# Merge stage of a hybrid encoder layer: stores one pass later, own buffers for three weight slabs, output-stage input in the raw weight buffers

## The chip, the core and the metric

The kernel runs on one core of a Trainium2 chip. The metric is device time in microseconds (us) of one execution, input and output in the chip's main memory (HBM). The engines are called as the profile calls them: PE multiplies matrices, DVE and POOL do elementwise work, ACT does activations and copies, and SP issues every transfer (DMA) that is spoken of here.

## What is computed

One layer of a streaming encoder, 2048 tokens of width 1024, all in 32-bit floats. Three branches (attention "fox", a state-space layer "s5", a cross-attention "mem") give gated outputs `y_fox`, `y_s5`, `y_mem`. The end of the layer is what this case is about:

```python
gates = sigmoid(gl + b_merge).reshape(Bn, L, N_BRANCH, D_MODEL)
merged = (gates[:, :, 0] * (y_fox @ w_proj_fox)
          + gates[:, :, 1] * (y_s5 @ w_proj_s5)
          + gates[:, :, 2] * (y_mem @ w_proj_mem))
x = x + merged @ w_out
return rms_norm(x, g_final)
```

To keep accuracy each 32-bit operand is split into a rounded part (hi) and the rest (lo), and each product is three matmuls: hi by hi, hi by lo, lo by hi.

## The kernel before

The tokens are cut into four chunks of 512 (c = 3, 2, 1, 0), the 1024 output channels into eight blocks of 128 (m). Between the stages everything lies in scratch tensors in HBM: `s_ys`, `s_ym`, `s_yx` are the three branches' outputs, `s_gl` the gates, `s_mg` the merged rows, `s_mp` a partial sum of chunk 3.

- **Chunk 3** (`gen_merge0`) is merged while the attention runs on, as filler for PE. It goes in two parts: part 0 merges s5 and mem into `s_mp`; part 1, when the attention is nearly over, adds the fox branch, with the partial loaded back (line 950), and stores to `s_mg` (line 953). Gates and reloaded partials share two buffers named `g`. Its last line loads chunk 2's ten `ys` and `ym` tiles through two raw buffers named `yr` and splits them (`merge_load`, line 905 for the load).
- **Chunks 2, 1, 0** (`merge_out`) follow in 24 passes, one per chunk and m. A pass has 48 matmuls of 128x512: 18 for s5 into a bank psB, 12 for mem into psC, 18 for fox into psA, with three weight slabs: two of 640 columns (`w_proj`, slabs 0 and 1) and one of 768 (`w_proj_x`). DVE multiplies each bank by its gate (line 977), POOL adds the three (lines 978, 979), SP stores the sum (line 980). Within the passes the next chunk's sixteen y tiles are loaded, and in chunk 0's passes `w_out` (line 990).
- **The output stage** takes 16 blocks of 128 tokens: load eight merged tiles `mt` (line 1000), split, 48 matmuls with `w_out` into psF and psA in turn, add the residual `xo` (line 1013), norm, store.

A slab is loaded by `load_w` into one of two raw buffers `wraw` (line 139), then split: hi by ACT or POOL (`split`, lines 891 and 893, chosen by the flag `hi_act`), lo by DVE (line 895). All three slabs of a pass go through the same two `wraw`; slabs 0 and 1 share two split buffers, the third has two of its own. `hi_act` is set at the start of `merge_out`.

The order on each engine is made at build time by a scheduler, which follows the program's order, the free buffers and its own estimate of durations. SP's list is one queue: a transfer that waits for a buffer or for a result holds back every transfer behind it.

Of the kernel before, what the change touches and what calls it, by code (L numbers as in the profile page):

```python
# [4 lines left out]
F32 = mybir.dt.float32  # L5
F32R = mybir.dt.float32r
# [6 lines left out]
D = 1024  # L13
L = 2048
NC = 4
CW = 512
KD = 8
# [10 lines left out]
NV = 268  # L28
# [21 lines left out]
class Layer:  # L50
# [863 lines left out]

    def merge_w(self, m, part, pool=None):
        return [self.load_w(self.i["w_proj"][2 * m + a], (5, 128)) for a in range(2)] if part == 0 else \
            [self.load_w(self.i["w_proj_x"][m], (6, 128), pool)]

    def gen_merge0(self):


        nc, s, c = self.nc, self.s, NC - 1
        self.yp, self.close_yp = self.pool("yp", side="left")
        self.ys = {q: [] for q in range(NC)}
        self.merge_load(c, self.SRC[:10], self.yp, self.yp)
        ys = self.ys[c]
        for part, brs in ((0, ((1, range(6)), (2, range(6, 10)))), (1, ((0, range(10, 16)),))):
            if part:
                while not self.ready:
                    yield  # L930
                self.merge_load(c, self.SRC[10:], self.yp, self.yp)
            for m in range(KD):
                ms = slice(m * 128, (m + 1) * 128)
                ws = self.merge_w(m, part)
                g = []
                for br, ks in brs:
                    t = self.merge_gate(self.yp, br, m, c, 2)
                    ps = self.psFA() if self.over else self.psF()
                    for kk in ks:
                        w = ws[0 if part else kk // 5]  # L940
                        q = (kk - 10) if part else kk % 5
                        self.mm3(ps, (w[0][:, q, :], w[1][:, q, :]), ys[kk], kk == ks[0], kk == ks[-1])
                        if kk % 2 and kk != ks[-1]:
                            yield
                    nc.vector.scalar_tensor_tensor(out=t, in0=t, scalar=1.0, in1=ps, op0=ALU.add, op1=ALU.mult)
                    g.append(t)
                    yield
                if part:
                    t = self.yp.tile([128, CW], F32, tag="g", name="g", bufs=2)
                    nc.sync.dma_start(out=t, in_=s["mp"][ms, :])  # L950
                    g.append(t)
                nc.gpsimd.tensor_add(g[0], g[0], g[1])
                nc.sync.dma_start(out=s["mg"][ms, c * CW:(c + 1) * CW] if part else s["mp"][ms, :], in_=g[0])
        self.merge_load(c - 1, self.SRC[:10], self.yp, self.yp)

    def merge_out(self):
        nc, s, i = self.nc, self.s, self.i
        p, close = self.pool("mrg", side="right")
        gfin = p.tile([128, D], F32, name="gfin")
        nc.sync.dma_start(out=gfin, in_=i["g_final"].partition_broadcast(128))  # L960
        yq, yp = p, self.yp
        self.hi_act = True
        pm, close_m = self.pool("mrw", side="right")
        self.merge_load(NC - 2, self.SRC[10:], yq, pm, 3)
        for c in range(NC - 2, -1, -1):
            ys = self.ys[c]
            for m in range(KD):
                ps = {0: self.psA(), 1: self.psB(), 2: self.psC()}
                ws = self.merge_w(m, 0) + self.merge_w(m, 1, pm)
                cnt = {0: 6, 1: 6, 2: 4}  # L970
                for kk, (n, k, br) in enumerate(self.SRC):
                    w, q = ws[min(kk // 5, 2)], kk - 5 * min(kk // 5, 2)
                    self.mm3(ps[br], (w[0][:, q, :], w[1][:, q, :]), ys[kk], k == 0, k == cnt[br] - 1)
                g = {}
                for br in (1, 2, 0):
                    t = g[br] = self.merge_gate(pm, br, m, c)
                    nc.vector.scalar_tensor_tensor(out=t, in0=t, scalar=1.0, in1=ps[br], op0=ALU.add, op1=ALU.mult)
                nc.gpsimd.tensor_add(g[1], g[1], g[2])
                nc.gpsimd.tensor_add(g[1], g[0], g[1])
                nc.sync.dma_start(out=s["mg"][m * 128:(m + 1) * 128, c * CW:(c + 1) * CW], in_=g[1])  # L980
                if c and m < KD - 1:
                    for e in self.SRC[m * 16 // 7:(m + 1) * 16 // 7]:
                        self.merge_load(c - 1, [e], yq if (e[0] == "yx") == (c == 1) else yp, pm, 3)
                elif m < KD - 1:
                    if m == 0:
                        wo, nw = {}, 0
                    for _ in range((8 * (m + 1)) // 7 - (8 * m) // 7):
                        n, q = nw // 4, nw % 4
                        raw = self.wp.tile([128, 4 * NV], F32, tag="wraw", name="wraw", bufs=2)
                        nc.sync.dma_start(out=raw[:, :1024], in_=i["w_out"][nw])  # L990
                        for a in range(2):
                            w = (yq if 2 * nw + a < 10 else yp).tile([128, 1024], F32R, tag="y", name="wo", bufs=16)
                            self.split(w[:, :512], w[:, 512:], raw[:, a * 512:(a + 1) * 512])
                            wo[n, 2 * q + a] = (w[:, :512], w[:, 512:])
                        nw += 1
        close_m()
        po, close_o = self.pool("mro", side="right")
        for t in [c * 4 + q for c in range(NC - 1, -1, -1) for q in range(4)]:
            m_c = po.tile([128, KD, 128], F32, tag="m", name="mt", bufs=2)
            nc.sync.dma_start(out=m_c, in_=s["mg"].rearrange("(k p) n -> p k n", p=128)[:, :, t * 128:(t + 1) * 128])  # L1000
            hi = self.wp.tile([128, KD, 128], F32R, tag="whi", name="whi", bufs=2)
            lo = self.wp.tile([128, KD, 128], F32R, tag="wlo", name="wlo", bufs=2)
            self.split(hi, lo, m_c)
            x = po.tile([128, D], F32, tag="x", name="xo", bufs=3)
            nc.sync.dma_start(out=x, in_=i["x"][t * 128:(t + 1) * 128, :])
            j = po.tile([128, D], F32, tag="j", name="jo", bufs=2)
            ssq, r = (po.tile([128, 2], F32, tag=q, name=q, bufs=2) for q in ("ssq", "rs"))
            for n in range(2):
                ns = slice(n * 512, (n + 1) * 512)
                ps = self.psFA()  # L1010
                for k in range(KD):
                    self.mm3(ps, (hi[:, k, :], lo[:, k, :]), wo[n, k], k == 0, k == KD - 1)
                nc.vector.scalar_tensor_tensor(out=x[:, ns], in0=ps, scalar=0.5, in1=x[:, ns], op0=ALU.mult, op1=ALU.add)
                nc.scalar.activation(j[:, ns], x[:, ns], AF.Square, accum_out=ssq[:, n:n + 1])
            nc.vector.tensor_add(ssq[:, 0:1], ssq[:, 0:1], ssq[:, 1:2])
            self.rsqrt(po, r[:, 0:1], ssq[:, 0:1], 1)
            for n in range(2):
                ns = slice(n * 512, (n + 1) * 512)
                nc.vector.scalar_tensor_tensor(out=j[:, ns], in0=x[:, ns], scalar=r[:, 0:1], in1=gfin[:, ns],
                                               op0=ALU.mult, op1=ALU.mult)  # L1020
                nc.sync.dma_start(out=self.out[t * 128:(t + 1) * 128, ns], in_=j[:, ns])
        close_o()
        close()
        self.close_yp()

    def run(self):
# [20 lines left out]
        for n, _ in enumerate(fox):  # L1047
            marks.append(self.pe)
            due += PACE
            while due >= 1.0:  # L1050
# [3 lines left out]
                        next(fill, None)  # L1054
                else:
                    next(fill, None)
        self.over = True
        for _ in fill:
            pass
        self.close_f()  # L1060
# [77 lines left out]
```

## Time and profile before

| | |
|---|---|
| time, median of 3 | 3053.83 us (3053.64 to 3059.55) |
| the profiled execution | 3062.09 us, its span 3060.3 us |
| granted PE clock, mean | 0.991 |
| DMA | 417.80 MB, mean 137 GB/s |

The views are read as follows. A table by stage gives the engines' busy time, with the number of instructions in brackets, the granted PE clock, the DMA engines' busy share and the rate. Since matmuls overlap, their number in a stage says more of PE than its busy time. The list of waits says who waited for whom. The chain of work is followed back from the last instruction; its pieces stand in order of time.

### The profile page before, as it was taken

What the parts mean: (1) busy time and instruction counts of PE and PEld (TensorE: products, weight loads), DVE (VectorE), ACT (ScalarE), POOL (GpSimd) and SP (SyncE); (2) the same over time, 40 slices, a digit from 0 to 9 for tenths busy, and PEclk for the clock granted to TensorE, in tenths of its full rate; (3) what the DMA queues carried; (4) which work ended last, traced back from release to release, by engine and by line L of the source; (5) the groups of instructions that cost most, each with busy time, mean ns of one, the idle gap of its engine ahead of it and who ended that gap; (6) DMA issues with size and microseconds to landing.
All of it is one profiled execution on the core that took longest, in us unless ns stands there. A gap on an engine that the chain in (4) does not pass through costs nothing.

```text
span 3060.3 us, 43643 instructions
## 1 busy us (share of the span) xinstructions
PE 2968.6 (97%) x14656; PEld 2420.4 (79%) x14656; DVE 1845.9 (60%) x4982; ACT 1030.9 (34%) x2023; POOL 877.9 (29%) x1186
## 2 busy tenths in 40 slices
PE   9999999999999999999999999999999998999899
PEld 7889977777777778888878888888887776777687
DVE  5333389899985763322217777777777886434344
ACT  5102111111112321222216666666666542222222
POOL 0010000000002432122116565556655763222100
PEclk9999999999999999999999999999999999999999
DMA  5343323323335655344353434444444548766542
GB/s 167 107 138 95 104 88 114 116 93 115 129 124 157 176 153 169 118 127 125 116 160 101 128 117 111 121 120 112 114 117 132 161 137 269 223 184 212 168 144 97
DMA packets 306671, 417.80 MB, mean 137 GB/s; under 512 B 84084, under 2 KB 165236, under 8 KB 306436
## 3 DMA queue, kind: packets, MB, share of 16 engines
q1 hardware_dynamic: 306160, 414.95, 45.4%
q8 instruction: 116, 1.90, 0.3%
q14 instruction: 107, 0.88, 0.1%
q10 hardware_dynamic: 288, 0.07, 0.0%
HBM read 276.00 MB, written 138.90 MB: 136 GB/s over the span
## 4 chain that ended last, share of the span: by engine, by line
PE 76%; DMA 10%; DVE 6%; issue 3%; POOL 3%; ACT 2%; SPq 1%; POOLq 0%; DVEq 0%; ACTq 0%
PE psF L147 10%; PE psF L148 10%; PE psF L149 10%; PE psA L148 7%; PE psA L147 7%; PE psA L149 7%; PE psC L799 5%; PE psB L783 5%; PE psA L752 2%; PE psA L751 2%; PE psC L149 2%; DMA wraw<-in_w_proj 2%; PE psC L148 2%; PE psC L147 2%; DMA wraw<-in_w_proj_x 1%
## 5 line engine op out<-in xcount | busy, mean ns | idle before, releaser
L147 PE MATMUL psF<-hh,whi 128*128 128x512 f32 (+1 forms) x1160 | 468.9, 404 | 5.4 <-DVE elo L228 2.5
L149 PE MATMUL psF<-hh,wlo 128*128 128x512 f32 (+1 forms) x1160 | 460.0, 397 | 0.0
L148 PE MATMUL psF<-hl,whi 128*128 128x512 f32 (+1 forms) x1160 | 459.5, 396 | 0.0
L895 DVE TENSOR_TENSOR wlo<-wraw,whi 128x1024 fp32r<-128x1024 f32 (+2 forms) x216 | 250.9, 1163 | 307.5 <-POOL whi L893 156.5
L893 POOL TENSOR_SCALAR whi<-wraw 128x1024 fp32r<-128x1024 f32 (+2 forms) x144 | 145.7, 1012 | 728.5 <-PE psA L148 315.3
L147 PE MATMUL psA<-hh,whi 128*128 128x512 f32 (+1 forms) x816 | 321.7, 396 | 1.7 <-ACT hh L187 1.0
L148 PE MATMUL psA<-hl,whi 128*128 128x512 f32 (+1 forms) x816 | 323.2, 396 | 0.0
L149 PE MATMUL psA<-hh,wlo 128*128 128x512 f32 (+1 forms) x816 | 321.1, 394 | 0.6 <-DVE wlo L895 0.6
L799 PE MATMUL psC<-Pt,v 128*128 128x512 f32 x864 | 266.5, 398 | 6.1 <-DVE Pt L787 4.2
L787 DVE TENSOR_TENSOR Pt<-psB,Pt 128x512 fp32r<-128x512 f32 x336 | 226.0, 685 | 73.3 <-ACT Pt L786 70.7
L147 PEld LDWEIGHTS psF<-hh,whi 128*128 128x128 f32 x1160 | 219.0, 189 | 52.1 <-DVE elo L228 3.3
L149 PEld LDWEIGHTS psF<-hh,wlo 128*128 128x128 f32 x1160 | 218.6, 188 | 51.3 <-issue 0.4
L148 PEld LDWEIGHTS psF<-hl,whi 128*128 128x128 f32 x1160 | 219.1, 189 | 45.8 <-issue 0.4
L753 DVE CUSTOM_DVE_ANT_0 P<-psA,nf 128x512 f32<-128x512 f32 (+1 forms) x336 | 201.4, 627 | 45.7 <-PE psA L752 26.5
L786 ACT CAST Pt<-psB 128x512 fp32r<-128x512 f32 x336 | 191.6, 586 | 96.2 <-PE psB L783 51.6
L762 POOL TENSOR_SCALAR P<-P,rd 128x768 f32<-128x768 f32 (+1 forms) x240 | 193.8, 824 | 57.2 <-DVE rd L759 36.4
L751 PE MATMUL psA<-kk,qh 128*128 128x512 f32 (+1 forms) x480 | 184.9, 390 | 6.0 <-DVE mx L753 3.6
L147 PEld LDWEIGHTS psA<-hh,whi 128*128 128x128 f32 x816 | 153.5, 189 | 37.1 <-POOL whi L893 1.8
L149 PEld LDWEIGHTS psA<-hh,wlo 128*128 128x128 f32 x816 | 153.9, 189 | 35.4 <-DVE wlo L895 0.8
L799 PEld LDWEIGHTS psC<-Pt,v 128*128 128x128 f32 x864 | 153.1, 189 | 34.9 <-DVE Pt L787 8.7
L148 PEld LDWEIGHTS psA<-hl,whi 128*128 128x128 f32 x816 | 154.0, 189 | 33.6 <-DVE hl L188 0.2
L783 PE MATMUL psB<-ident,P 128*128 128x128 f32 x1200 | 176.9, 274 | 0.3 <-POOL P L762 0.2
(356 smaller groups left out, 6193.8 us busy)
## 6 DMA issues: line engine op xcount, KB each, us to landing
wraw<-in_w_in SPq DMA_DIRECT2D x90, 512.0 KB, 4.2
s_gl<-ehi SPq DMA_DIRECT2D x96, 256.0 KB, 2.6
g<-s_gl SPq DMA_DIRECT2D x96, 256.0 KB, 4.8
wraw<-in_w_proj SPq DMA_DIRECT2D x64, 320.0 KB, 3.3
s_vs<-ev_v SPq DMA_DIRECT2D x48, 256.0 KB, 2.7
nf<-s_nf SPq DMA_DIRECT2D x24, 512.0 KB, 6.7
v<-s_vs SPq DMA_DIRECT2D x24, 512.0 KB, 6.2
qh<-s_qh SPq DMA_DIRECT2D x96, 128.0 KB, 3.9
```

What stands on the lines that cost most here:

```text
L147: nc.tensor.matmul(out, a[0], b[0], start=first, stop=False)
L148: nc.tensor.matmul(out, a[0], b[1], start=False, stop=False)
L149: nc.tensor.matmul(out, a[1], b[0], start=False, stop=last)
L751: nc.tensor.matmul(ps[:, :wm], q[0][:, qs], kk[:, c0:c0 + wm], start=True, stop=False)
L753: nc.vector.tensor_tensor_reduce(out=pr[:, c * 512:c * 512 + w], in0=ps[:, :w], in1=nf[:, c0:c0 + w], scale=1.0, scalar=-3.0e38, op0=ALU.a ...
L762: nc.gpsimd.tensor_scalar(out=c, in0=c, scalar1=rd, scalar2=0.5, op0=ALU.mult, op1=ALU.mult)
L783: nc.tensor.transpose(ps[:, o:o + 128], P[b][:, kt * 128:(kt + 1) * 128], self.ident)
L786: nc.scalar.copy(hi, psv)
L787: nc.vector.tensor_sub(lo, psv, fl32(hi))
L799: self.pe = nc.tensor.matmul(o, v, m, start=(kt == 0), stop=(kt == 2 * G + 1))
L893: self.nc.gpsimd.tensor_scalar(out=hi, in0=x, scalar1=sc, scalar2=1.0, op0=ALU.mult, op1=ALU.mult)
L895: self.nc.vector.tensor_sub(lo, x, fl32(hi))
```

## The change

`merge_out` gets its slabs from a new function: slab 0 as before by `wraw`, slabs 1 and x through two raw buffers of their own (`raw`) into split buffers of their own, two for each slab. Its sums are stored by `store()` at the end of the next pass. It has six gate buffers in place of five, and two `yr` buffers in place of three. `gen_merge0` stores part 1's sums one m later, and loads the partials back into `yr` in place of `g`. `hi_act` is set when the attention ends, before the rest of `gen_merge0` is written. The tiles `mt` use the `wraw` buffers, and `gfin` is loaded at the start of the output stage.

```diff
+    def merge_ws(self, m, p):
+        ws = [self.load_w(self.i["w_proj"][2 * m], (5, 128))]
+        for src, k, t in ((self.i["w_proj"][2 * m + 1], 5, "b"), (self.i["w_proj_x"][m], 6, "x")):
+            raw = p.tile([128, 768], F32, tag="raw", name="raw", bufs=2)[:, :k * 128]
+            self.nc.sync.dma_start(out=raw, in_=src)
+            hi, lo = (p.tile([128, k * 128], F32R, tag=n + t, name=n + t, bufs=2) for n in ("hi", "lo"))
+            self.split(hi, lo, raw)
+            ws.append(tuple(x.rearrange("p (k m) -> p k m", k=k) for x in (hi, lo)))
+        return ws
...
 # gen_merge0
-                    t = self.yp.tile([128, CW], F32, tag="g", name="g", bufs=2)
+                    t = self.yp.tile([128, CW], F32, tag="yr", name="yr", bufs=2)
                     nc.sync.dma_start(out=t, in_=s["mp"][ms, :])
...
-                nc.sync.dma_start(out=s["mg"][ms, c * CW:(c + 1) * CW] if part else s["mp"][ms, :], in_=g[0])
+                if last:
+                    nc.sync.dma_start(out=last[0], in_=last[1])
+                if part:
+                    last = s["mg"][ms, c * CW:(c + 1) * CW], g[0]
+                else:
+                    nc.sync.dma_start(out=s["mp"][ms, :], in_=g[0])
+        nc.sync.dma_start(out=last[0], in_=last[1])
         self.merge_load(c - 1, self.SRC[:10], self.yp, self.yp)
...
 # merge_out
-        gfin = p.tile([128, D], F32, name="gfin")
-        nc.sync.dma_start(out=gfin, in_=i["g_final"].partition_broadcast(128))
-        self.hi_act = True
-        self.merge_load(NC - 2, self.SRC[10:], yq, pm, 3)
+        self.merge_load(NC - 2, self.SRC[10:], yq, pm)
...
-                ws = self.merge_w(m, 0) + self.merge_w(m, 1, pm)
+                ws = self.merge_ws(m, pm)
...
-                    t = g[br] = self.merge_gate(pm, br, m, c)
+                    t = g[br] = self.merge_gate(pm, br, m, c, 6)
...
-                nc.sync.dma_start(out=s["mg"][m * 128:(m + 1) * 128, c * CW:(c + 1) * CW], in_=g[1])
+                store()
+                last = slice(m * 128, (m + 1) * 128), slice(c * CW, (c + 1) * CW), g[1]
...
+        store()
         close_m()
         po, close_o = self.pool("mro", side="right")
+        gfin = po.tile([128, D], F32, name="gfin")
+        nc.sync.dma_start(out=gfin, in_=i["g_final"].partition_broadcast(128))
...
-            m_c = po.tile([128, KD, 128], F32, tag="m", name="mt", bufs=2)
+            m_c = self.wp.tile([128, 4 * NV], F32, tag="wraw", name="mt", bufs=2)[:, :1024].rearrange("p (k n) -> p k n", k=KD)
...
 # run
-        self.over = True
+        self.over = self.hi_act = True
         for _ in fill:
             pass
```

**SP, one pass of chunk 1**, without y loads, before:

```order
L980 DMA s_mg<-g 128x512
L912 DMA g<-s_gl 128x512 x2
L139 DMA wraw<-in_w_proj_x 128x768
L139 DMA wraw<-in_w_proj 128x640
L912 DMA g<-s_gl 128x512
L139 DMA wraw<-in_w_proj 128x640
```

And of the change, where `raw` are the new raw buffers:

```order
L983 DMA s_mg<-g 128x512
L912 DMA g<-s_gl 128x512 x2
L139 DMA wraw<-in_w_proj 128x640
L924 DMA raw<-in_w_proj 128x640
L912 DMA g<-s_gl 128x512
L924 DMA raw<-in_w_proj_x 128x768
```

The number of transfers is the same. The store in the list is now that of an earlier pass, and two of the three slabs have left `wraw`.

**SP, the turn from chunk 3 to chunk 2**, with buffer numbers, which rise with the place in the program: before, `yr_26302` to `yr_26347` are chunk 2's ten `ys` and `ym` tiles, and `g_26074` is the first of chunk 3's eight partials that is loaded back.

```order
L905 DMA yr_26312<-s_ys_133 128x512
L905 DMA yr_26317<-s_ys_133 128x512
L139 DMA wraw_26110<-in_w_proj_x 128x768
L808 DMA s_yx_131<-oo_25859 64x256
L773 DMA gf_25941<-s_gf_122 64x256
L905 DMA yr_26322<-s_ys_133 128x512
L905 DMA yr_26327<-s_ys_133 128x512
L953 DMA s_mp_135<-g_25976 128x512
L912 DMA g_26052<-s_gl_124 128x512
L139 DMA wraw_26142<-in_w_proj_x 128x768
L950 DMA g_26074<-s_mp_135 128x512
```

Of the change: `yr_26297` is the last of the partials, `yr_26302` chunk 2's first `ys` tile and `yr_26307` to `yr_26327` the other five; `yr_26470` to `yr_27031` are chunk 1's tiles.

```order
L961 DMA yr_26297<-s_mp_135 128x512
L139 DMA wraw_26665<-in_w_proj 128x640
L924 DMA raw_26671<-in_w_proj 128x640
L905 DMA yr_26561<-s_ys_133 128x512
L905 DMA yr_26566<-s_ys_133 128x512
L912 DMA g_26275<-s_gl_124 128x512
L965 DMA s_mg_136<-g_26243 128x512
L905 DMA yr_26302<-s_ys_133 128x512
L905 DMA yr_26652<-s_ys_133 128x512
L905 DMA yr_26657<-s_ys_133 128x512
L970 DMA s_mg_136<-g_26275 128x512
L905 DMA yr_26307<-s_ys_133 128x512
```

Chunk 2's `ys` tiles stood ahead of the first reloaded partial and now stand behind the last one, with pairs of chunk 1's tiles between them; `yr_26327`, the sixth, stands two further pairs of chunk 1's tiles below the last row shown. PE's list has turned to fit: between the last run of five attention matmuls (line 799) and the first matmul into psB there were 156 merge matmuls, and now there are 228, since the fox sums of three passes and the whole of chunk 3 stand ahead of psB.

**SP, the end of the merge**, before:

```order
L990 DMA wraw<-in_w_out 128x1024
L980 DMA s_mg<-g 128x512
L139 DMA wraw<-in_w_proj 128x640
L912 DMA g<-s_gl 128x512 x2
L139 DMA wraw<-in_w_proj 128x640
L139 DMA wraw<-in_w_proj_x 128x768
L912 DMA g<-s_gl 128x512
L980 DMA s_mg<-g 128x512 x2
L1000 DMA mt<-s_mg 128x8x128
```

Of the change:

```order
L1023 DMA mt<-s_mg 128x8x128
L912 DMA g<-s_gl 128x512
L983 DMA s_mg<-g 128x512
L912 DMA g<-s_gl 128x512 x2
L1023 DMA mt<-s_mg 128x8x128
L983 DMA s_mg<-g 128x512
L1023 DMA mt<-s_mg 128x8x128
L983 DMA s_mg<-g 128x512
L1020 DMA gfin<-in_g_final 128x1024
L1028 DMA xo<-in_x 128x1024 x3
```

Three `mt` loads (and a fourth, further up) have moved ahead of the last store; `gfin` and the residuals `xo` stay behind it.

More of the change, by code (lines that the diff above doesn't have):

```diff
@@ L916, in merge_w @@
         return [self.load_w(self.i["w_proj"][2 * m + a], (5, 128)) for a in range(2)] if part == 0 else \
-            [self.load_w(self.i["w_proj_x"][m], (6, 128), pool)]
+            [self.load_w(self.i["w_proj_x"][m], (6, 128))]
+    def merge_ws(self, m, p):
[7 more added lines that the diff above has]
+        return ws
     def gen_merge0(self):
@@ L925, in gen_merge0 @@
         self.merge_load(c, self.SRC[:10], self.yp, self.yp)
-        ys = self.ys[c]
+        ys, last = self.ys[c], None
         for part, brs in ((0, ((1, range(6)), (2, range(6, 10)))), (1, ((0, range(10, 16)),))):
@@ L958, in merge_out, with store @@
         p, close = self.pool("mrg", side="right")
-        gfin = p.tile([128, D], F32, name="gfin")
-        nc.sync.dma_start(out=gfin, in_=i["g_final"].partition_broadcast(128))
         yq, yp = p, self.yp
-        self.hi_act = True
         pm, close_m = self.pool("mrw", side="right")
-        self.merge_load(NC - 2, self.SRC[10:], yq, pm, 3)
+        self.merge_load(NC - 2, self.SRC[10:], yq, pm)
+        last = None
+        def store():
+            if last:
+                nc.sync.dma_start(out=s["mg"][last[0], last[1]], in_=last[2])
         for c in range(NC - 2, -1, -1):
@@ L979, in merge_out @@
                 nc.gpsimd.tensor_add(g[1], g[0], g[1])
-                nc.sync.dma_start(out=s["mg"][m * 128:(m + 1) * 128, c * CW:(c + 1) * CW], in_=g[1])
+                store()
+                last = slice(m * 128, (m + 1) * 128), slice(c * CW, (c + 1) * CW), g[1]
                 if c and m < KD - 1:
                     for e in self.SRC[m * 16 // 7:(m + 1) * 16 // 7]:
-                        self.merge_load(c - 1, [e], yq if (e[0] == "yx") == (c == 1) else yp, pm, 3)
+                        self.merge_load(c - 1, [e], yq if (e[0] == "yx") == (c == 1) else yp, pm)
                 elif m < KD - 1:
```

## The prediction, made before the changed kernel was run

> **What bounds the kernel.** First the page, for the span and the engine that fills it:
>
> ```profile
> span 3060.3 us, 43643 instructions
> PE 2968.6 (97%) x14656; PEld 2420.4 (79%) x14656; DVE 1845.9 (60%) x4982; ACT 1030.9 (34%) x2023; POOL 877.9 (29%) x1186
> ```
>
> PE bounds the whole, so a change can only win where PE stands still. The second view is the table by stage, over the part that the change touches:
>
> ```profile
> 2340.00:2520.00 180.00, 166.13 (x860) 132.76 (x858) 149.36 (x374) 94.00 (x199) 126.29 (x168) 0.99 0.51 149
> 2520.00:2560.00 40.00, 29.52 (x102) 21.64 (x103) 19.97 (x23) 4.51 (x8) 17.07 (x19) 0.87 0.74 249
> 2560.00:2620.00 60.00, 56.02 (x233) 42.74 (x233) 39.10 (x48) 21.18 (x31) 18.55 (x13) 1.00 0.87 286
> 2620.00:2840.00 220.00, 209.40 (x867) 162.89 (x866) 99.74 (x134) 57.01 (x81) 54.22 (x36) 0.98 0.68 200
> 2840.00:2880.00 40.00, 27.12 (x105) 20.75 (x104) 13.98 (x17) 7.58 (x10) 6.42 (x5) 0.87 0.61 193
> 2900.00:3000.00 100.00, 100.00 (x431) 80.74 (x431) 45.04 (x106) 23.48 (x54) 0.00 (x0) 1.00 0.45 142
> ```
>
> The last row is PE without a gap: 431 matmuls of 128x512 in 100 us, 0.232 us each. From 2520 on every merge matmul has this shape, so a stage's loss is its length less its count times 0.232: 40 − 23.7 = 16.3, 60 − 54.1 = 5.9, 220 − 201.1 = 18.9, 40 − 24.4 = 15.6. The turn from chunk 3 to chunk 2 (2520 to 2620) loses **22.2 us**, the passes **18.9**, the step into the output stage **15.6**: 56.7 us is the most the merge can give. The output stage itself loses nothing. The third view says what PE waits for after 2280:
>
> ```profile
> PE psB L147 <- ACT whi L891: 10.0, 7, 3.1
> PE psF L147 <- ACT whi L891: 9.6, 1, 9.6
> PE psA L147 <- POOL whi L893: 6.4, 3, 5.1
> PE psA L149 <- DVE wlo L895: 4.1, 10, 1.3
> ```
>
> Total, times and longest: split weights, nearly always. The 9.6 is the output stage's first `mt`.
>
> **The passes.** One pass in the chain of work, in order of time:
>
> ```profile
> 2733.93 0.69 DVE g L977
> 2734.76 1.75 POOL g L979
> 2736.53 2.23 DMA s_mg<-g
> 2739.21 4.97 DMA wraw<-in_w_proj_x
> 2744.20 0.85 ACT whi L891
> ...
> 2745.95 0.69 DVE g L977
> ```
>
> It goes round in 12.02 us where 48 matmuls need 11.1. The store waits for POOL, the gate loads behind it wait for the store to land, and only then does SP issue the next slab. The SP queue's own waits say the same for 2540 to 2870:
>
> ```profile
> SPq L139 <- DVE wlo L895: 53.0, 35, 4.8
> SPq L980 <- POOL g L979: 46.9, 22, 5.4
> ```
>
> The change stores a sum a pass later, so POOL's add is long done when SP reaches it; and slabs 1 and x have raw buffers freed a pass or more before use. The number of transfers, splits and matmuls stays. What is late next is the gate: pass m's first gate reuses a buffer of pass m−2, whose store goes out about 3 us into pass m−1 and takes 2.2; with 5 us to land the gate is there 10 us into m−1, and psB of pass m ends 15 us after that pass's start. So 5 us of cover; if SP is held longer than that, each pass pays the excess. DMA has room: 220 us at 200 GB/s squeezed into 201 is 219, below the 286 of the turn. Two `yr` buffers in place of three bind only in the turn: in chunk 1's passes sixteen loads spread over seven passes. I keep 1 us of 18.9: **gain 18**, with ends 6 (a third, if held) and 18.9.
>
> **The step into the output stage.**
>
> ```profile
> 2862.33 0.70 DVE g L977
> 2863.14 1.30 POOLq L1134
> 2864.45 2.00 DMA s_mg<-g
> 2866.52 4.10 DMA mt<-s_mg
> 2870.72 1.06 ACT whi L891
> ...
> 2871.83 0.79 PE psF L147
> xo<-in_x SPq DMA_DIRECT2D x4, 512.0 KB, 6.0
> gfin<-in_g_final SPq DMA_DIRECT2D x1, 512.0 KB, 6.5
> ```
>
> The last two rows are from the DMA issues (KB each, median us to landing). The last merge matmul ends at T = 2862.25; sum, store, `mt` and split follow one another while PE stands. In `wraw`, and for chunk 3's tokens first, `mt` no longer waits for that store. Late next is `xo`: behind the last store, which lands at T + 4.2, come `gfin` and `xo`, there at about T + 4.7 + 6.5 = T + 11.2, and its sum into psF ends 0.7 later. PE needs psF again after 48 matmuls, T + 11.1. That leaves a wait of 1 (0 to 4, if the four 512 KB transfers share the engines), and the gap in the last pass goes too. **Gain 14** of 15.6; ends 6 (only the 9.6 is halved) and 15.6.
>
> **The turn.** It is the part that may go either way.
>
> ```profile
> 2512.24 0.97 PE L799 MATMUL psC<-Pt,v 128*128 128x512 f32 x4
> wraw<-in_w_proj_x SPq DMA_DIRECT2D x11, 384.0 KB, 5.5
> yr<-s_ys SPq DMA_DIRECT2D x13, 256.0 KB, 4.3
> yr<-s_ym SPq DMA_DIRECT2D x8, 256.0 KB, 4.1
> L891 ACT ACTIVATE ymg<-yr 128x512 fp32r<-128x512 f32 x38 | 23.7, 630 | 60.0 <-DMA yr<-s_yx 23.8 <-POOL ymg L893 16.5 <-DMA yr<-s_ys 10.3
> L895 DVE TENSOR_TENSOR ymg<-yr,ymg 128x512 fp32r<-128x512 f32 x39 | 31.4, 823 | 15.8 <-ACT ymg L891 15.8
> ```
>
> For it: gates and partials of chunk 3 no longer share two buffers, its stores come later, and hi goes from POOL to ACT, so the longest wait above (5.1 on POOL) should go. Against it: chunk 2's y tiles can be loaded only when chunk 3's last two sums have freed `yr`, in pairs, in one queue with chunk 1's. PE's list covers part: from 2513 its 228 merge matmuls take 53 us and the last attention work 3, so a dense PE is at psB at 2569 and misses the sixth `ys` tile at 2572. Chunk 3's last-but-one sum is 18 + 24 matmuls earlier, 2559, plus 2.5 for gate and add: first `ys` issue at 2561.5, the second, after the last sum, at 2566. A round of two loads takes 4.2 to land, 0.63 + 0.63 + 0.82 to split, 6.2 us. Loads two and three go at 2566, four and five at 2572, the sixth at 2578, ready at 2584: a wait of 12. The wave of `w_proj_x` and fox tiles ahead of it costs some 4 (by SP's list about 19 MB from 2513 up to the sixth tile, at 286 GB/s 66 us, so 2579 and not 2578 for its landing, and less where SP waits), and psC's last tile 2. I take 18 lost in place of 22.2: **gain 4**. Ends: 4 lost (the loads land a round earlier; gain 18), and 40 lost (two more rounds of 8 and another 6; gain −18).
>
> A single long wait costs more than itself:
>
> ```profile
> 2540.00:2550.00 10.00, 7.13 (x18) 5.19 (x19) 4.54 (x6) 1.84 (x3) 1.42 (x2) 0.66 1.02 352
> ```
>
> Behind the 5.1 us wait the granted clock was 0.66 over ten us. The Trainium skill, "TensorE: Matmul & The Clock Gate", Part 1, has the clock at half after an idle window of about 3.4 us, until as much busy time has passed; this row agrees. By that rule the wait of 12, if in one piece, would add 1.7 to 3.4 us, and in pieces under 3.4 nothing: the sum would end up to 3 us higher.
>
> **The attention's end (2340 to 2520).** Setting the flag early moves the splits of chunk 3's six fox tiles from POOL to ACT there, and four of chunk 2's leave.
>
> ```profile
> PE psF L147 <- POOL ymg L893: 3.4, 3, 2.5
> L895 DVE TENSOR_TENSOR wlo<-wraw,whi 128x640 fp32r<-128x640 f32 x15 | 22.5, 1498 | 1.1 <-POOL whi L893 1.1
> L895 DVE TENSOR_TENSOR wlo<-wraw,whi 128x640 fp32r<-128x640 f32 x38 | 32.8, 864 | 27.2 <-ACT whi L891 27.2
> ACT ymg L891 <- DMA yr<-s_yx: 23.8, 12, 6.1
> ```
>
> The same DVE subtraction takes 1498 ns beside a busy POOL (2340 to 2520) and 864 where ACT makes hi (2620 to 2860). PE's list is also reordered, which no row can price. I take **2 us** gained, with ends −10 and +8. The Trainium skill, "GPSIMD Engine Reference", section 1, says that POOL shares its SBUF interfaces with DVE and collides with instructions that read two SBUF inputs; the two means agree. By it ten splits fewer on POOL would free about ten times 0.6 us of DVE, 6 in place of 2 if all lay on the path.
>
> **The sum.** 18 + 14 + 4 + 2 = 38 us. The profiled execution took 3062.09 us (1.8 around its span), which becomes 3024; it stands 8.3 above the median of the runs, 3053.83, which I take off: **3016**.
>
> **Rivals.**
> - *The turn gives the gain back.* Rounds of 8 us and chunk 3's sums 8 later lose 35 instead of 18: 3016 + 17 = 3033. For it: the order of SP. Against: the landing times above were taken in a stretch at 250 to 286 GB/s, and pairs of 256 KB move less.
> - *The y tiles are hidden.* 4 lost: 3002.
> - *The store was not what held the slabs*, so the change doesn't do its main work: slab 0 and `w_out` still share `wraw`, passes stay at 12.0, gain 38 − 18: 3034. The chain above speaks against it.
> - *Slower: ACT as the attention's gate.* PE's Pt tiles come from ACT in order; six y splits and some four slab splits now stand in its list before the last of them, each waiting for a DMA. The longest such wait above is 6.1 us; ten exposed give 61, less 36 won elsewhere: 3079. It decides once the ten cost 3.6 us each. Against it: ACT was busy 94 of 180 us and the mean of that wait is 2.
>
> **Chances.** Forecast (3008 to 3026) 0.62, turn 0.17, hidden 0.10, no main work 0.05, ACT 0.06 (of which 0.04 beyond the old time). Range 2996 to 3041: the forecast, both turns and the third rival; 0.12 is left out. About 0.2% (6 us) is what a measurement of this kernel can tell. Faster by more than that 0.92, within it 0.04, slower 0.04.
>
> **What would show it.** Right: passes of about 11.1 us with no wait on `whi`; PE going from the merge to `wo` matmuls within 2 us; one wait of PE in front of psB for `ymg`, 10 to 20 us in all. Wrong: SP waiting for gates' buffers with PE waiting on DVE's gate product; PE waiting for Pt with ACT behind `yr`; over 25 us lost in front of psB. The forecast falls if the passes stay at 12 us, or if the attention's end grows by more than 10.

## The result, and the profile after

The changed kernel takes 3036.11 us (median; 3032.29 to 3038.93 over its runs), 3053.83 before on the same chip: ratio 0.9937, 95% interval 0.9918 to 0.9955. It is faster by 18 us, half of the 38 us forecast. That is inside the range, 20 above the forecast and outside the stretch 3008 to 3026 that had been given 0.62.

The page of the profiled execution, and the stages, with the columns of the table by stage before:

```profile
span 3030.5 us, 43647 instructions
PE 2956.7 (98%) x14656; PEld 2424.2 (80%) x14656; DVE 1842.2 (61%) x4982; ACT 1044.1 (34%) x2049; POOL 864.8 (29%) x1160
...
2340.00:2520.00 180.00, 169.66 (x866) 138.03 (x865) 142.05 (x365) 98.92 (x208) 119.75 (x158) 0.97 0.52 154
2520.00:2560.00 40.00, 30.92 (x123) 23.66 (x123) 19.65 (x24) 13.15 (x19) 7.16 (x5) 0.91 0.93 305
2560.00:2620.00 60.00, 47.74 (x185) 35.86 (x183) 35.55 (x47) 21.64 (x34) 12.05 (x8) 0.94 0.71 229
2620.00:2820.00 200.00, 195.23 (x839) 158.25 (x838) 109.50 (x140) 57.49 (x85) 61.78 (x37) 0.99 0.72 228
2820.00:2860.00 40.00, 40.00 (x175) 32.48 (x173) 12.62 (x22) 7.48 (x11) 7.64 (x6) 1.00 0.50 158
```

Length less count times 0.232, as before: the turn loses 11.5 + 17.1 = 28.6 us (22.2 before), the passes 200 − 194.6 = 5.4 (18.9 before), the step into the output stage nothing (15.6 before). So the two gains came and the turn went the wrong way. PE's waits after 2280:

```profile
PE psA L147 <- ACT whi L891: 8.0, 1, 8.0
PE psB L147 <- ACT ymg L891: 5.4, 3, 2.9
PE psC L147 <- DVE g L996: 4.8, 2, 4.2
PE psA L147 <- ACT hix L891: 3.9, 1, 3.9
```

Of the four, three stand in the turn; the third is mainly one gap of 4.2 us in the passes. Of the eleven waits for `whi` in the list before (7, 1 and 3) one is left, beside one of 3.9 and one of 1.5 for the new slabs' `hix` and `hib`.

**One measure for all runs.** The stages shift between kernels, so the experiments are compared between marks in each trace: from 2340 to the last attention matmul; from there to DVE's last gate product of chunk 2's second pass (the turn); from there to that of the 23rd pass (the passes); from there to 40 us past the first `w_out` matmul (the step). A loss is again the time between two marks less 0.232 us for each 128x512 matmul started there (less for narrower ones, by their width). A pause of PE that runs across a mark is counted whole in the stage where it begins; in the change this is the wait of 3.9 us for `hix`, which ends at 2607.2. The first and the last of these marks in the change (start, us, engine and line, what), the two between being 2605.1 and 2833.3:

```profile
2513.18 0.52 PE L799 MATMUL psC<-Pt,v 128*128 128x512 f32 x2
...
2844.16 0.40 PE L147 MATMUL psF<-wo,whi 128*128 128x512 f32 x1
```

The losses in us, with the time of the profiled execution and the median and ratio of each kernel's runs (ratio to the runs of before on the same chip and in the same series; their medians were 3058.29 us for `e1` to `e5`, 3058.98 for `a_again` and `e6` to `e8`, 3059.82 for `b_again` and `e9` to `e11`):

| kernel | att. end | turn | passes | step | profiled | median | ratio, 95% interval |
|---|---|---|---|---|---|---|---|
| before | 36.9 | 20.4 | 26.3 | 12.0 | 3062.09 | 3053.83 | |
| before, again (`b_again`) | 37.8 | 17.2 | 24.1 | 12.5 | 3060.59 | 3059.68 | 0.9995, 0.9986 to 1.0003 |
| the change | 33.1 | 28.6 | 7.3 | 0.1 | 3032.29 | 3036.11 | 0.9937, 0.9918 to 0.9955 |
| the change, again (`a_again`) | 32.3 | 31.1 | 11.0 | 0.1 | 3038.53 | 3038.94 | 0.9933, 0.9917 to 0.9949 |
| `e1_slabs` | 37.9 | 12.8 | 4.3 | 14.9 | 3039.97 | 3038.80 | 0.9941, 0.9929 to 0.9953 |
| `e2_store` | 37.1 | 18.0 | 29.2 | 12.3 | 3062.98 | 3064.84 | 1.0024, 1.0012 to 1.0036 |
| `e3_mt` | 35.3 | 31.2 | 8.9 | 15.0 | 3053.81 | 3057.62 | 0.9999, 0.9990 to 1.0007 |
| `e5_hiact` | 35.6 | 27.8 | 12.4 | 0.1 | 3040.50 | 3042.20 | 0.9955, 0.9943 to 0.9967 |
| `e6_merge0` | 33.6 | 13.1 | 7.2 | 0.1 | 3018.27 | 3015.22 | 0.9863, 0.9846 to 0.9879 |
| `e7_ysfirst` | 35.1 | 15.2 | 5.2 | 0.1 | 3024.39 | 3016.60 | 0.9869, 0.9850 to 0.9889 |
| `e8_wout` | 32.9 | 12.3 | 4.2 | 0.1 | 3013.85 | 3020.03 | 0.9878, 0.9859 to 0.9898 |
| `e9_mpyr` | 34.6 | 31.6 | 9.2 | 0.1 | 3040.95 | 3040.95 | 0.9937, 0.9925 to 0.9949 |
| `e10_best` | 35.3 | 10.7 | 5.5 | 0.1 | 3017.72 | 3016.87 | 0.9858, 0.9843 to 0.9873 |
| `e11_now` | 34.4 | 9.6 | 6.6 | 0.1 | 3016.76 | 3022.55 | 0.9875, 0.9860 to 0.9890 |

Two executions of one kernel differ by up to 3.7 us in a stage; less than that is not read from this table.

### The profile page after: what moved, and what is told of

Read it like the earlier page. It is cut to its first block, busy times and chain, and to the rows that moved or that the text cites. A ratio compares the mean times of both kernels' runs of the same rounds, so it can differ in the third digit from the quotient of the medians.

```text
span 3030.5 us, 43647 instructions
## 1 busy us (share of the span) xinstructions
PE 2956.7 (98%) x14656; PEld 2424.2 (80%) x14656; DVE 1842.2 (61%) x4982; ACT 1044.1 (34%) x2049; POOL 864.8 (29%) x1160
## 4 chain that ended last, share of the span: by engine, by line
PE 80%; DMA 9%; DVE 5%; issue 3%; POOL 2%; ACT 1%; SPq 0%; DVEq 0%; POOLq 0%; ACTq 0%
PE psF L147 10%; PE psF L148 10%; PE psF L149 10%; PE psA L149 8%; PE psA L147 8%; PE psA L148 8%; PE psC L799 6%; PE psB L783 5%; PE psA L752 3%; PE psA L751 3%; PE psC L147 2%; PE psC L149 2%; PE psC L148 2%; DMA wraw<-in_w_out 1%; DMA yr<-s_ys 1%
## 5 line engine op out<-in xcount | busy, mean ns | idle before, releaser
L893 POOL TENSOR_SCALAR whi<-wraw 128x1024 fp32r<-128x1024 f32 (+2 forms) x134 | 137.0, 1023 | 710.3 <-PE psA L148 307.0
L895 DVE TENSOR_TENSOR wlo<-wraw,whi 128x1024 fp32r<-128x1024 f32 (+2 forms) x168 | 204.9, 1221 | 191.8 <-POOL whi L893 152.5
```

Of the source, the lines that this page charges most:

```text
L893: self.nc.gpsimd.tensor_scalar(out=hi, in0=x, scalar1=sc, scalar2=1.0, op0=ALU.mult, op1=ALU.mult)
L895: self.nc.vector.tensor_sub(lo, x, fl32(hi))
```

## The experiments

### What the slabs and the store each do

`e1_slabs` is the kernel before with the slabs' own buffers alone. For room, `gfin` moves to the output stage, as in the change; the store stays where it was.

```diff
-                ws = self.merge_w(m, 0) + self.merge_w(m, 1, pm)
+                ws = self.merge_ws(m, pm)
```

> The kernel before with one part of the change: slabs 1 and x have raw and split buffers of their own (gfin is loaded in the output stage to make room); each sum is still stored in its own pass. A pass took 12.0 us before, and 24 passes lost about 19 us between 2620 and 2840. Theory A (the store at the head of SP's queue holds the slabs back): passes stay at 11.7 to 12.0 us, 13 to 19 us lost, ratio 0.997 to 1.000. Theory B (two raw buffers for three slabs are what binds): passes near 11.1 us, under 5 us lost, ratio 0.994 or less. Both: the step into the output stage still costs 12 us or more, the turn from chunk 3 to chunk 2 about 22.

`e2_store` is the kernel before with the later store in `merge_out` alone:

```diff
-                    t = g[br] = self.merge_gate(pm, br, m, c)
+                    t = g[br] = self.merge_gate(pm, br, m, c, 6)
...
-                nc.sync.dma_start(out=s["mg"][m * 128:(m + 1) * 128, c * CW:(c + 1) * CW], in_=g[1])
+                store()
+                last = slice(m * 128, (m + 1) * 128), slice(c * CW, (c + 1) * CW), g[1]
```

> The kernel before with the other part: sums of chunks 2 to 0 stored a pass later, with six gate buffers; all three slabs still through two raw buffers. Theory A: passes of 11.1 to 11.3 us, under 6 us lost between 2620 and 2840 where 19 were, ratio 0.994 to 0.996. Theory B: passes stay at 11.7 to 12.0, 13 us or more lost, ratio 0.997 to 1.000. Both: the step into the output stage still costs 12 us or more.

The slabs alone give 0.9941, as much as the whole change, and bring the passes' loss from 24–26 us to 4.3. They help the turn too, which was not expected: it loses 12.8 us, where 22 had been expected and the kernel before loses 17.2 and 20.4. The later store alone gives 1.0024: if anything slower, the passes lose 29.2. Why a store a pass later frees nothing stands in SP's waits (us, times, longest) in eight passes, 2690 to 2790. Before:

```profile
SPq L139 <- DMA wraw<-in_w_proj_x: 26.1, 8, 4.2
SPq L980 <- POOL g L979: 16.5, 8, 2.2
```

With the later store alone:

```profile
SPq L139 <- DMA wraw<-in_w_proj_x: 25.8, 8, 3.9
SPq L969 <- POOL g L984: 16.5, 8, 2.2
```

The rows are the same to 0.3 us. SP, POOL and a gate's path stand so in one of its passes:

```profile
2720.94 1.76 POOL L984 TENSOR_TENSOR g<-g 128x512 f32<-128x512 f32 x1 [8.93 <-DVE g L982]
...
2722.72 0.33 SPq L969 DMA_DIRECT2D s_mg<-g  x1
2723.10 2.29 SPq L912 DMA_DIRECT2D g<-s_gl  x2
2725.50 0.38 SPq L139 DMA_DIRECT2D wraw<-in_w_proj_x  x1
...
2734.77 0.33 SPq L969 DMA_DIRECT2D s_mg<-g  x1
```

The store goes out 0.02 us after POOL's sum, the next pass's 12.05 us later, and gates and slabs wait behind it as before. SP's list, as built, says why. The numbers rise with the place in the program, and are 1 or 2 apart between these kernels for the same thing. Before, with the later store, and with the slabs alone:

```
L980 DMA s_mg_136<-g_27836 128x512
L139 DMA wraw_27946<-in_w_proj 128x640

L969 DMA s_mg_136<-g_27835 128x512
L139 DMA wraw_27945<-in_w_proj 128x640

L989 DMA s_mg_136<-g_27834 128x512
L912 DMA g_28004<-s_gl_124 128x512
L139 DMA wraw_28116<-in_w_proj 128x640
```

In the first two the same sum is stored ahead of the same slab. The store is written a pass later, and the scheduler lists it where it was: the slabs behind it could not go earlier, since they had no buffer. In the third, slabs stand some two passes further on (numbers rise by about 90 a pass) behind the same store. SP's waits there:

```profile
SPq L912 <- DMA s_mg<-g: 17.6, 8, 3.3
...
SPq L989 <- POOL g L988: 7.1, 9, 0.8
```

SP holds still, 17.6 us for gate buffers and 7.1 for the sums, and PE no longer notices. From 2690 to 2810 PE's only wait is this one, at 2806:

```profile
PE psC L147 <- DVE g L986: 3.8, 1, 3.8
```

So what bound the passes was three slabs through two raw buffers. `e1_slabs` gives slabs 1 and x their own split buffers as well, and no run parts the two. But from 2690 to 2790 of the kernel before, ACT's splits waited 73.5 us for slabs to land and once, 4.3 us, for PE to free a split buffer.

`e11_now`, run later, asks the same from the other side: the change with chunk 3's merge as before (`e6_merge0`, below) and the sums of the passes stored at once.

```diff
-                store()
                 last = slice(m * 128, (m + 1) * 128), slice(c * CW, (c + 1) * CW), g[1]
+                store()
```

> The changed kernel with chunk 3's merge as before and the passes' sums stored at once, so that of the change the three slabs' own buffers, the output stage's slabs in the raw buffers and the later setting of nothing else are left. Theory R (two raw buffers for three slabs bind, and the later store is worth nothing): 3013 to 3018 us, passes 3 to 24 losing 5 to 9 us. Theory Q (the later store is needed beside the slabs): passes 3 to 24 lose 15 us or more and the time is 3024 or more.

The passes lose 6.6 us, with the later store 7.2, and the ratios, 0.9875 and 0.9863, have overlapping intervals. Beside the slabs too the later store is worth nothing that these runs show. The median, 3022.55, lies between the times that the two theories gave; the passes' loss decides for theory R.

### The output stage's input

`e3_mt` is the change with `mt` in two buffers of its own again, in the pool that opens after the last store:

```diff
-            m_c = self.wp.tile([128, 4 * NV], F32, tag="wraw", name="mt", bufs=2)[:, :1024].rearrange("p (k n) -> p k n", k=KD)
+            m_c = po.tile([128, KD, 128], F32, tag="m", name="mt", bufs=2)
```

> The changed kernel, with the output stage's first tiles again in buffers of the output stage's own pool. If loading them ahead of the last store is what closed the step, PE waits for the first of them again, 9 to 11 us, the stage loses 11 to 13 us where the change lost none, and the time is 11 to 13 us above the changed kernel's, about 3048. Rival: the step closed because the last sums are added and stored sooner; then under 4 us come back.

The whole gain is gone: 0.9999. PE's longest wait is back, and longer than the 9.6 before (`e1_slabs`, where `mt` has its own buffers too, also has 12.2):

```profile
PE psF L147 <- ACT whi L891: 12.2, 1, 12.2
```

The step loses 15.0 us in place of 0.1. Between the two kernels' profiled executions there are 15.3 us (3053.81 and 3038.53 for `a_again`), between the medians 18.7; the 3 us more were not located.

### The turn

`e5_hiact` is the change with the flag `hi_act` set at the start of `merge_out`, as before:

```diff
+        self.hi_act = True
...
-        self.over = self.hi_act = True
+        self.over = True
```

> The changed kernel, with the flag that sends the hi copies to ACT set at the start of the merge of chunks 2 to 0 again, so that chunk 3's last splits are POOL's. Theory: the flag is worth little, 0 to 4 us, at the attention's end (2340 to 2520 loses about 35 us either way, in the changed kernel 35.4) and the turn (2520 to 2620) loses 26 to 32 us as in the change (28.6). Rival 1: ACT's list, with y splits that wait for transfers, is what made the turn worse: the turn loses 22 or less. Rival 2: POOL was the limit in the turn: it loses 34 or more.

The time is 0.9955 (interval 0.9943 to 0.9967) where the change has 0.9933 and 0.9937 in two other series; the intervals overlap, so what the flag is worth, some 6 us by the medians' ratios, isn't settled. The turn loses 27.8, as in the change. It isn't the flag.

`e6_merge0` is the change with `gen_merge0` as before: partials back in `g`, sums stored at once.

```diff
-                    t = self.yp.tile([128, CW], F32, tag="yr", name="yr", bufs=2)
+                    t = self.yp.tile([128, CW], F32, tag="g", name="g", bufs=2)
...
-                if last:
-                    nc.sync.dma_start(out=last[0], in_=last[1])
...
+                nc.sync.dma_start(out=s["mg"][ms, c * CW:(c + 1) * CW] if part else s["mp"][ms, :], in_=g[0])
```

> The changed kernel with chunk 3's merge as before: partials reloaded into the gates' buffers, sums stored at once, chunk 2's ten ys and ym loads no longer behind the partials. Theory (the loads behind the partials, and chunk 1's loads between them, cost the turn): the turn loses 20 to 24 us where the change loses 28.6, and no wait for ymg stands in front of psB; time 3 to 8 us below the changed kernel's. Rival (the turn is bound by transfers, whatever their order): it loses 26 to 30.

`e7_ysfirst` keeps the change's `gen_merge0` and only writes the loading of chunk 2's `ys` and `ym` tiles ahead of part 1, so ahead of the partials:

```diff
             if part:
...
                 self.merge_load(c, self.SRC[10:], self.yp, self.yp)
+                self.merge_load(c - 1, self.SRC[:10], self.yp, self.yp)
...
-        self.merge_load(c - 1, self.SRC[:10], self.yp, self.yp)
```

> The changed kernel with one line moved: chunk 2's ys and ym tiles are loaded ahead of chunk 3's second part and its partials, since the ys and ym tiles of chunk 3 are free by then. Theory as for the kernel with the old chunk 3 merge: the wait for ymg in front of psB (some 9 us with its pieces) goes, the turn loses 14 to 22 us, time 6 to 14 us below the changed kernel's, about 3026. Rival (transfers bind): the wait moves to the slabs (whi or hix), the turn loses 26 to 30 and the time is the changed kernel's.

`a_again` is the change itself beside them:

> The changed kernel as it is, a second time: ratio within 0.9918 to 0.9955, and a second profile, to see how far the stages' losses repeat: 2340 to 2520 35 us, turn 28.6, passes 5.4, step into the output stage none; each within 3 us, if they are the program's and not the run's.

In that series the change has 3038.94 us, `e6_merge0` 3015.22 and `e7_ysfirst` 3016.60. The edits of `gen_merge0` cost 24 us, and one line that changes only the order of the loads gives 22 of them back. `e9_mpyr` leaves one of the two edits: the partials in `yr`, the sums stored at once.

```diff
-                if last:
-                    nc.sync.dma_start(out=last[0], in_=last[1])
...
+                nc.sync.dma_start(out=s["mg"][ms, c * CW:(c + 1) * CW] if part else s["mp"][ms, :], in_=g[0])
```

> The changed kernel with chunk 3's sums stored at once again, its partials still loaded into the two yr buffers. Theory P (the partials share the two yr buffers, so chunk 2's y tiles come late): as slow as the change, 3036 to 3041 us, the turn losing 25 to 30 us from the last attention matmul to the end of chunk 2's second pass. Theory S (the stores a pass later are what holds SP's queue): 3015 to 3020, the turn losing 13, as with the whole of chunk 3's merge put back.

It has 0.9937 and loses 31.6 us in the turn, like the change. So the partials in `yr` do it, not the later store. The DMA issues (operation, count, KB each, median us to landing) from 2505 to 2530 show how. With chunk 3's merge as before (`e6_merge0`):

```profile
yr<-s_ys SPq DMA_DIRECT2D x4, 256.0 KB, 5.1
yr<-s_ym SPq DMA_DIRECT2D x4, 256.0 KB, 3.2
```

In the change no such row stands in that window. Its loads come in one wave, from 2552 to 2580:

```profile
yr<-s_ys SPq DMA_DIRECT2D x12, 256.0 KB, 3.6
yr<-s_ym SPq DMA_DIRECT2D x4, 256.0 KB, 3.7
```

The two `yr` buffers go round in program order: chunk 2's tiles, written behind the eight partials, can't be loaded before the last partial is freed by the last sum. With chunk 3's merge as before, such loads slip into the attention's end, where the core of `e6_merge0` moved 114 GB/s (2460 to 2505) and 250 (2505 to 2530). PE's pieces in the change's turn (start, us, what, and in brackets the wait ahead of it):

```profile
2543.59 0.79 PE L147 MATMUL psA<-ymg,whi 128*128 128x512 f32 x1 [7.98 <-ACT whi L891]
2568.34 0.73 PE L147 MATMUL psB<-ymg,whi 128*128 128x512 f32 x2 [2.14 <-ACT ymg L891]
2573.82 0.74 PE L147 MATMUL psB<-ymg,whi 128*128 128x512 f32 x2 [2.94 <-ACT ymg L891]
2599.58 0.50 PE L147 MATMUL psB<-ymg,hib 128*128 128x512 f32 x1 [1.49 <-ACT hib L891]
2607.21 0.50 PE L147 MATMUL psA<-ymg,hix 128*128 128x512 f32 x1 [3.91 <-ACT hix L891]
```

The second and third are the `ys` tiles, 5 us; with the shorter waits beside them and a slower clock behind them (last section), the stretch from 2565.6 to 2584.9 loses 10. The last two are slabs of chunk 2's third and fourth pass. The chain of work there, in order of time, runs through the late y tiles into the slab:

```profile
2592.65 4.97 DMA yr<-s_yx
2597.64 0.64 ACT ymg L891
...
2600.25 1.94 DVE lob L895
2602.20 4.08 DMA raw<-in_w_proj_x
2606.31 0.85 ACT hix L891
2607.21 0.50 PE psA L147
```

The first, 8 us, is chunk 3's last fox slab; how it was held:

```profile
2528.68 0.63 ACT L891 ACTIVATE ymg<-yr 128x512 fp32r<-128x512 f32 x1 [6.82 <-DMA yr<-s_yx]
2529.74 0.83 ACT L891 ACTIVATE whi<-wraw 128x768 fp32r<-128x768 f32 x1
...
2533.31 0.85 ACT L891 ACTIVATE whi<-wraw 128x768 fp32r<-128x768 f32 x1 [1.38 <-DMA wraw<-in_w_proj_x]
...
2534.41 0.37 SPq L139 DMA_DIRECT2D wraw<-in_w_proj_x  x1
...
2542.70 0.84 ACT L891 ACTIVATE whi<-wraw 128x768 fp32r<-128x768 f32 x1 [1.97 <-DMA wraw<-in_w_proj_x]
```

ACT stood 6.8 us on a fox tile of chunk 2 with a slab's split behind it in its list, and the last slab goes into that slab's raw buffer; then it took 8 us to land, in the stretch 2520 to 2560 above, where DMA is 0.93 busy. In `e6_merge0` PE's longest wait in this place is 4.4 us, in `e9_mpyr` 8.1; by which of the two links, ACT's or the landing's, was not separated.

Yet this wait is not what the shared `yr` costs. Cut the turn behind chunk 3's last matmul (2556.3 in the change), with losses in us:

| kernels | up to chunk 3's last matmul | behind it |
|---|---|---|
| before, twice, and `e2_store` | 19.1, 16.0, 17.7 | 1.2, 1.3, 0.3 |
| the change, twice | 12.8, 13.4 | 15.9, 17.8 |
| `e3_mt`, `e5_hiact`, `e9_mpyr` (partials in `yr`, loads behind them) | 14.0, 13.4, 14.5 | 17.4, 14.5, 16.9 |
| `e1_slabs`, `e6_merge0`, `e10_best`, `e11_now` (partials in `g`) | 12.8, 13.2, 10.8, 9.7 | 0.0 in all |
| `e7_ysfirst`, `e8_wout` (loads ahead of the partials) | 15.3, 12.4 | 0.0 in both |

In the kernels with the slabs' own buffers the first part, 9.7 to 15.3 us, doesn't go by where the partials lie. The second part is there, beyond 1.3 us, only where chunk 2's tiles are loaded behind partials in `yr`: in the change 10 us on the tiles and 5.9 on the two slabs.

### One `w_out` tile per pass

The gap of 4.2 us in the passes stands in front of psC with DVE's gate product late. Chunk 0's passes load eight `w_out` tiles in seven passes, two in the seventh. `e8_wout` (on `e7_ysfirst`) and `e10_best` (on `e6_merge0`) load one in each of eight:

```diff
-                elif m < KD - 1:
+                elif not c:
...
-                    for _ in range((8 * (m + 1)) // 7 - (8 * m) // 7):
+                    for _ in range(1):
```

> As the kernel with the line moved, and w_out is loaded one tile a pass over eight passes, where the seventh pass had two. Theory: the 4.2 us wait of psC for a gate product in chunk 0's seventh pass, behind the second tile's split in DVE's list, goes; the passes lose under 1 us and the time is 4 to 6 us below that of the kernel with the line moved alone. Rival: the last tile, now a pass later, holds the output stage's first second half: the same 4 us are lost there.

> The changed kernel with chunk 3's merge as before and one w_out tile loaded in each of chunk 0's eight passes in place of two in the seventh. If the 4.1 us gap near 2798 us in the run with chunk 3's merge as before comes from two w_out tiles sharing wraw in one pass, that gap falls to 1 or 2 and the time is 3011 to 3013 us. If the gap is the gate product's own place in DVE's list, it stays and the time is 3014 to 3017.

Nothing is gained: 0.9878 beside 0.9869 for `e7_ysfirst`, 0.9858 beside 0.9863 for `e6_merge0`. In `e8_wout` the gap fell from 4.2 us to 2.1, with one of 0.9 behind it, and the time did not follow. In `e10_best` it stays, 3.5 us at 2810. DVE's list ahead of it:

```profile
2804.05 1.29 DVE L895 TENSOR_TENSOR wo<-wraw,wo 128x512 fp32r<-128x512 f32 x2 [8.30 <-ACT wo L891]
...
2808.53 0.67 DVE L990 SCALAR_TENSOR_TENSOR g<-g,psB 128x512 f32<-128x512 f32 x1
2809.13 0.68 DVE L990 SCALAR_TENSOR_TENSOR g<-g,psC 128x512 f32<-128x512 f32 x1
```

One `w_out` tile is enough: its split, for which DVE stood 8.3 us, and two slabs' behind it are listed ahead of the products that free psB and psC. The second tile in one pass was at most a part of the cause.

`e6_merge0` and `e10_best` are the fastest of all runs and beat both kernels: 1.4% faster than before (0.9863 and 0.9858), 0.7% faster than the change.

### The kernel before once more

> The kernel before, unchanged, profiled again. It tells how much of the 29.8 us between the two profiled executions (3062.09 and 3032.29) is the change and how much is the spread of single executions, since the medians differ by 17.7 only. If the spread lies in the merge stage (in places that the change removed), another profiled execution nearer the median loses some 8 us less from 2340 to the first wo matmul than the 95.7 us of the first profile. If it lies ahead of it, the first merge matmul is earlier than 2359.5 us by as much and the losses behind it are the same within 3 us.

Its second profile is 1.5 us shorter than the first, so it doesn't lie 8 nearer the first median. The median itself moved: 3053.83 in the first series, 3058 to 3060 in the three later ones, and 3059.68 here. And the change's first profile, 3032.29, is the fastest of that series' five runs. The 29.8 us between the first two profiles are thus some 20 of the change (0.9933 to 0.9937) and 10 of spread; the second pair lies 22 apart.

## Why the prediction was right and wrong

By the mean of the two pairs in the table, before less after: passes +16, step +12, turn −11, attention's end +5. Together 22; the prediction had 38.

- **The passes: 18 predicted, 16 measured. The size held, the first reason did not.** The prediction had the store as what holds SP and the slabs. The later store alone left SP's list and its waits as they were. What it named second, "slabs 1 and x have raw buffers freed a pass or more before use", does all of it (`e1_slabs`, 4.3 lost). Its rival "the store was not what held the slabs" was right on the mechanism, and wrong to conclude that the passes stay at 12.0: slab 0 and `w_out` share `wraw` without harm. The signs it asked for came, one pass in 11.08 us by the stores, and no PE wait on `whi` in the passes:

```profile
2719.33 0.33 SPq L983 DMA_DIRECT2D s_mg<-g  x1
...
2730.41 0.33 SPq L983 DMA_DIRECT2D s_mg<-g  x1
```

- **The step: 14 predicted, 12 measured by these marks, 15.6 by the prediction's window.** `mt` leaves the path and PE goes on without a pause (its last merge matmul starts at 2843.92, the first `w_out` matmul at 2844.16). The wait of 1 us for `xo` did not come.
- **The attention's end: 2 predicted, 5 measured.** All runs with the flag set early lose 32.3 to 35.3 us here, those with it set late 35.6 to 37.9. One of the prediction's reasons shows: DVE's subtraction for 128x640 slabs takes 1177 ns on the mean there, 1498 before and 1464 in `e5_hiact`, where the flag is set late:

```profile
L895 DVE TENSOR_TENSOR wlo<-wraw,whi 128x640 fp32r<-128x640 f32 x15 | 17.7, 1177 | 1.8 <-POOL whi L893 1.5 <-ACT whi L891 0.3
```

  Fifteen of them save 4.8 us of DVE. By the Trainium skill, "GPSIMD Engine Reference", section 1, that the prediction weighed, this is the expected direction.
- **The turn: +4 predicted, −11 measured. This is the step that failed.** The prediction let the whole old loss go ("the longest wait above (5.1 on POOL) should go") and put 18 us for chunk 2's y tiles in its place. (By its own window the turn went from 22.2 lost to 28.6, −6.4.) The size of the 18 was nearly right: behind chunk 3's last matmul the change loses 15.9 and 17.8, in the first of the two 10 on the tiles and 5.9 on the slabs of two later passes. But up to that matmul 12.8 and 13.4 us stay of the 16.0 to 19.1 before; the wait of 5.1 on POOL became one of 8.0 on ACT. These 13 us had been put at nothing.

  The order of the loads was right, and the sixth `ys` tile, forecast for 2578, went out at that time:

```profile
2578.55 0.32 SPq L905 DMA_DIRECT2D yr<-s_ys  x1
```

  The microsecond is luck: the first two loads went at 2563.3 and 2569.5, 2 to 3.5 us late, and from the second to the sixth it took 9 us and not 12. PE's own time was luck too. The prediction let 228 merge matmuls start at 2513 and had PE at psB at 2569. In the trace 56 of them had run by then, and PE, 13 us in arrears from chunk 3, was done with the rest at 2566.2. The rival "the turn gives the gain back" had the sign, 35 us lost and 3033; 28.6 and 31.1 were measured. Its slower rounds of loads did not come.
- **The offset of 8.3 us** between profile and median was taken off, which is the same as taking 38 us from the median of 3053.83. Later series have 3058 to 3060 for the kernel before, so some 5 us of the offset belong to that first series and not to the kernel. Of the 20 us between forecast and result, the turn makes 15, passes and step 2 each, and the attention's end gives 3 back; the other 4 were not located.

## What to carry to other kernels

Count the buffers that a stream goes through before looking at what delays a transfer in the queue: three slabs a pass through two buffers set the pace here, and a store written later did nothing, since without a free buffer the scheduler had nothing to put ahead of it. When a buffer set is shared with a new use, look at whose loads had been running ahead in it for free. When one wait of a stage is to go, don't count the stage's other losses as gone with it. And the median of a few runs can itself stand some 5 us off, as it did here.

## What the hardware showed that was not expected

- **Waits of PE slowed the work behind them.** After PE's wait of 8.0 us the granted clock (the third number from the end) was 0.72 for 6.4 us, in which 21 matmuls ran:

```profile
2543.60:2550.00 6.40, 6.40 (x21) 5.10 (x22) 3.52 (x4) 1.59 (x2) 1.29 (x1) 0.72 1.00 372
```

  At 0.232 us they would take 4.9: 1.5 us on top, counted in the turn. By the Trainium skill, "TensorE: Matmul & The Clock Gate", Part 1, a wait past about 3.4 us has such a price, and the row agrees. So does the wait of 3.9: from 2608.4 to 2612.0 the clock was 0.53. But after the wait of only 2.9 us it was 0.59 from 2573.8 to 2578.0, and ten matmuls took 4.2 us, 1.9 more than at 0.232. The prediction had expected nothing of pieces under 3.4.
- **A 384 KB slab took longer to land in a crowd.** The DMA issues of the change from 2505 to 2530, where the core moved 225 GB/s, and from 2530 to 2552, at 323 GB/s:

```profile
wraw<-in_w_proj_x SPq DMA_DIRECT2D x5, 384.0 KB, 4.3
...
wraw<-in_w_proj_x SPq DMA_DIRECT2D x1, 384.0 KB, 8.2
```

  The second row is a single load. Loads of the same size into `raw` took 6.3 us (one) in the first stretch and 7.0 (median of two) in the second.
